# A decoder block on one core: VectorE issues in the order of the program text from step 40 to step 172

## The chip, the cores and the metric

The kernel runs on one core of one Trainium2 chip. Time is the device time of one execution in microseconds (us), taken over several executions; for the kernel before there are three, and one more that was profiled. The engines are named as the profile names them: PE is TensorE (PEld its weight loads), DVE is VectorE, ACT is ScalarE, POOL is GpSimd, SP is SyncE, whose queue issues most DMAs.

## The reference

One decoder layer on 256 tokens of width 2048, all in float32. The input is normalised and projected once; the projected columns feed two mixers that run side by side.

```python
h = rms_norm(x, g_mix); proj = h @ w_in                       # 2048 -> 8272 columns
u, z_ssm, c_q, k, v, z_attn, k_idx, w_idx, gate_ssm, gate_attn = split(proj)
y_ssm = s5_branch(u, ...) * silu(z_ssm)                        # diagonal complex state, a scan over 256 positions,
o_ssm = y_ssm @ w_ssm_out                                      #   then GELU and a gated projection (w_glu)
cq = rms_norm(c_q); q = cq @ w_uq; q_idx = cq @ w_uq_idx
y_attn = dsa_branch(q, k, v, q_idx, k_idx, w_idx) * silu(z_attn)   # 64 keys of 256 per query by an indexer's score
o_attn = y_attn @ w_attn_out
x = x + (sigmoid(gate_ssm) * o_ssm + sigmoid(gate_attn) * o_attn) @ w_o
x = x + sigmoid(rms_norm(x) @ w_ple_gate) * rms_norm(p @ w_ple)
return rms_norm(x, g_final)
```

## The kernel before, in words

**Units.** All weights stream through the core once. The stream is cut into 255 units of 128 partitions x 1024 columns (672 for eight of them), numbered in the order in which the products need them: 0 to 15 for `u`, 16 to 31 for `z_ssm`, 32 to 63 for `gate_ssm`, 64 to 79 for `z_attn`, 80 to 103 for three quarters of `gate_attn`, 104 to 115 for `c_q` and `k`, 116 to 123 for `v` and the indexer's key, 124 to 131 for `w_uq` and `w_uq_idx`, 132 to 147 for `w_glu`, 148 to 155 for the rest of `gate_attn`, 156 to 171 for `w_ssm_out`, from 172 for `w_attn_out`, and so on to `w_ple_gate`.

**Three products per weight.** A float32 product is made from three faster ones. A unit is loaded as `raw` by the SP queue (L99, five buffers). ACT rounds it to `hi` (`unit_hi`, L261, four buffers). DVE makes the remainder `lo` = `raw` - `hi` (`unit_lo`, L273, four buffers). PE then multiplies hi by hi, hi by lo and lo by hi into one accumulator (`mm3`, or `block_tm` with 512 columns per matmul: 12 matmuls per unit).

**One step per unit.** The main loop at L1225 writes step s in this order: the matmuls of unit s, `unit_hi(s + 3)`, the deferred evacuations of PSUM of earlier units (`run_deferred`), `unit_lo(s + 2)`, the load of the next unit, and then some work of the side threads (`pump(BUDGET)`, L33: about 1.3 us of DVE work per step by the threads' own estimates).

**The side threads** do what is no stream of weights. `s5_gen` (L939) is the scan: two halves of 16 state tiles each, `E[0]` in slot S7 and `E[1]` in slot S1. A half has 19 complex multiply-adds of four DVE instructions each (`cmadd`: L951, L953, L955, L957), so the scan has 152 DVE instructions. After a half, `s5_out` lets PE form the outputs (tile `aux`), DVE add the skip term (L998), ACT take the GELU (L1006) and round it (L1008), and DVE form the remainder (L1011). `attn_gen` scores keys (ACT L1034, DVE L1040 and L1042), picks 64 of them (L1049, L1050), forms logits (L1067) and their maximum (L1070), lets ACT take exponentials (L1073), divides on DVE (L1075, L1077), and at the end of it, head by head, multiplies with `za_d` loaded into `zld` (two buffers, L1104, L1086) and splits the product into hi and lo (ACT L1089, DVE L1092).

**Evacuations on DVE.** L438 scales a finished `z` block by the row of 1/rms; ACT then takes its SiLU (L442). L461, L470 and L472 do the same for `c_q`, L544 for the queries, L564, L566 and L568 for `w_glu`.

**What sets the order.** The program text only says what depends on what. A scheduler replays it with its own estimates of duration and writes one queue for each engine; each queue is then issued strictly in its order, with a semaphore wait where an operand comes from another engine. So an instruction that waits holds everything behind it on its engine. The scheduler may put a thread's DVE work far ahead of the step in which the text has it, and it did so with the scan.

Of the kernel before, what the change touches and what calls it, by code (L numbers as in the profile page):

```python
# [29 lines left out]
NC = 4  # L30
CW = 512
OFF = 16
NWARM = 30  # L33
BUDGET = 1.3
TRLAG = 2
# [9 lines left out]
def block_kernel(ctx: ExitStack, tc: tile.TileContext, A: dict, out: bass.AP):  # L45
# [18 lines left out]
    def slot(tag, shape, dt=F32):  # L64
        return cp.tile(shape, dt, tag=tag, name=nm(tag))

    def const(s, shape, dt=F32):
        return cp.tile(shape, dt, tag=s, name=s)
# [19 lines left out]
    def issue_unit(between=None):  # L88
        n = dma_next[0]
        if n >= len(units):  # L90
            return
        c, h, cols = units[n][:3]
        kind, idx = chunks[c]
        r = wp.tile([P, 1024], F32, tag="raw", name=nm("raw"), bufs=5)
        src = (A["wts"][idx] if kind == "w" else A["wvk"][idx])[:, h * cols:(h + 1) * cols]
        q = 2 if between else 1
        for i in range(q):
            s = slice(i * cols // q, (i + 1) * cols // q)
            nc.sync.dma_start(r[:, s], src[:, s])  # L99
            if between and i == 0:  # L100
                between()
        raws[n] = r
        dma_next[0] += 1
# [36 lines left out]
    def mm(o, l, r, start=True, stop=True, **kw):  # L140
        PE.matmul(o, l, r, start=start, stop=stop, **kw)  # L141
# [51 lines left out]
    def run_deferred(flush=False):  # L193
        while True:
            due = [d for d in deferred if flush or d[0] <= step[0]]
            if not due:
                return
            for d in due:
                deferred.remove(d)
            for d in due:  # L200
                d[1]()
# [26 lines left out]
    def pump(budget):  # L228
        credit[0] = min(credit[0] + budget, 3.0)
        while credit[0] > 0:  # L230
            ready = [t for t in threads if t[1] <= step[0]]
            if not ready:
                return
            credit[0] -= advance(ready[0])

    def drain(t):
        while not t[2]:
            advance(t)
# [13 lines left out]
    def unit_hi(u):  # L252
        if u >= len(units):
            return
        cols = units[u][2]
        hi = unit_tile("hi", u)
        src = raws[u][:, :cols]
        q = 2 if u < 3 else 1
        for i in range(q):
            o = slice(i * cols // q, (i + 1) * cols // q)  # L260
            S.copy(hi[:, o], src[:, o])  # L261
        his[u] = hi

    def unit_lo(u):
        if u >= len(units):
            return
        cols = units[u][2]
        lo = unit_tile("lo", u)
        src = raws.pop(u)
        q = 2 if u < 3 else 1  # L270
        for i in range(q):
            o = slice(i * cols // q, (i + 1) * cols // q)
            TT(lo[:, o], src[:, o], his[u][:, o].bitcast(F32), ALU.subtract)  # L273
        los[u] = lo
# [94 lines left out]
    def big_slot(tag, off=0):  # L369
        t = slot(tag, [P, KT * T + OFF], F32R)  # L370
        return t[:, off:off + KT * T].rearrange("p (k t) -> p k t", t=T)
# [254 lines left out]
    def ev_o(nb):  # L626
# [9 lines left out]
        def f(h, ps):  # L636
            if nb == 0 and h == 0:
                R["x2"] = slot("S1", [P, 2, D])
                R["x2h"] = big_slot("XH", OFF)
                R["x2l"] = big_slot("XL", OFF)  # L640
                R["sq2"] = const("sq2", [P, 2, NC])
# [373 lines left out]
    def attn_gen():  # L1015
# [63 lines left out]
        yield ("lag", 1)  # L1079
        ya = big_slot("S7", OFF).rearrange("p (c h) t -> p c h t", c=2)  # L1080
        R["ya"] = ya
# [128 lines left out]
    S.activation(first, mhalf, AF.Copy)  # L1210
    for i in range(NWARM):
        mm(wps[:, :T], warm[:, :P], warm)
# [9 lines left out]
    for i in range(2):  # L1222
        issue_unit()
    NU = len(units)
    for s in range(NU):  # L1225
        step[0] = s
        fn, need = units[s][3:]
        for n in need or ():
            if callable(n):
                n()  # L1230
            else:
                run_deferred()
                drain(R[n])
        fn(his.pop(s), los.pop(s))
        unit_hi(s + 3)
        run_deferred()
        unit_lo(s + 2)
        issue_unit()
        pump(BUDGET)
# [120 lines left out]
```

## Time and profile before

| what | value |
|---|---|
| three executions | 788.07, 788.10, 790.91 us (median 788.10) |
| the profiled execution | 790.16 us, of which the span from the first to the last instruction is 788.3 us |
| granted PE clock, mean over the span | 0.997 |
| PE busy | 766.6 us, 97% of the span |
| DVE busy | 576.5 us, 73% |
| ACT busy | 392.1 us, 50% |
| DMA, mean over the span | 201 GB/s |

A busy time is the union of the instructions of an engine. A matmul's record overlaps the next one's, so PE's busy time hides short losses; the distance from one matmul's start to the next tells more. "[2.27 <-DVE lo L273]" behind an instruction says that its engine was idle for 2.27 us before it, and that what ended the wait was an instruction of DVE at line 273 that writes `lo`.

### The profile page before, as it was taken

Reading aid. Unit: us, or ns where it says so; the run is one execution under the profiler, and the core shown is the slowest. Engines: PE = TensorE matmul, PEld = TensorE weight load, DVE = VectorE, ACT = ScalarE, POOL = GpSimd, SP = SyncE. Lnnn points to the kernel's source line nnn. Section 1 sums busy time; section 2 is a strip of 40 time slices with the busy share of each in tenths; the row PEclk is TensorE's granted clock in tenths of the full one; section 3 lists DMA queues with packets and bytes.
Section 4 is the critical chain, followed back from the end, with each engine's and each line's share of the span. In section 5 each row is a group of like instructions: output and inputs, shape, how many; then the busy total and the mean of one; then the engine's idle time right before and its main releaser. Section 6 shows DMA issues by size and latency. Waiting matters only on the chain.

```text
span 788.3 us, 12920 instructions
## 1 busy us (share of the span) xinstructions
PE 766.6 (97%) x5080; PEld 668.2 (85%) x5080; DVE 576.5 (73%) x902; ACT 392.1 (50%) x539; POOL 8.5 (1%) x18
## 2 busy tenths in 40 slices
PE   8999999999999899999999999999999999999995
PEld 6999987786998778899998987887888888888885
DVE  5999953999999964463768988665777855556753
ACT  7544456443433564453645474544446454455642
POOL 0000000000000000000000000000000000000000
PEclk9999999999999999999999999999999999999998
DMA  8768765355665376653664646775875765555622
GB/s 317 274 216 233 239 210 186 111 184 190 220 199 178 125 256 219 216 170 110 226 199 156 207 147 223 248 244 174 287 221 191 261 228 191 184 180 197 213 88 107
DMA packets 52637, 158.08 MB, mean 201 GB/s; under 512 B 5984, under 2 KB 12128, under 8 KB 52192
## 3 DMA queue, kind: packets, MB, share of 16 engines
q1 hardware_dynamic: 47392, 150.15, 57.9%
q10 hardware_dynamic: 5184, 7.10, 2.5%
q8 instruction: 40, 0.66, 0.4%
q14 instruction: 21, 0.17, 0.1%
HBM read 147.79 MB, written 8.39 MB: 198 GB/s over the span
## 4 chain that ended last, share of the span: by engine, by line
PE 47%; issue 1%; DMA 1%; DVE 1%; ACT 0%; POOLq 0%; POOL 0%; DVEq 0%
PE main L141 43%; PE aux L141 3%; PE aux L149 1%; DMA zld<-za_d 1%; DVE t L1086 0%; ACT S L669 0%; DVE S L667 0%; DVE S L668 0%; ACT S L664 0%; DVE S L671 0%; POOLq L1355 0%; POOL r3v L719 0%; DVE S L728 0%; DVEq L1355 0%; DVE S L726 0%
## 5 line engine op out<-in xcount | busy, mean ns | idle before, releaser
L273 DVE TENSOR_TENSOR lo<-raw,hi 128x1024 fp32r<-128x1024 f32 (+2 forms) x255 | 305.2, 1199 | 150.9 <-ACT hi L261 150.8
L261 ACT CAST hi<-raw 128x1024 fp32r<-128x1024 f32 (+2 forms) x255 | 261.6, 1033 | 285.4 <-PE main L141 240.0
L141 PE MATMUL main<-hi,S 128*128 128x512 f32 x512 | 162.6, 393 | 0.0
L141 PE MATMUL main<-lo,XH 128*128 128x512 f32 (+2 forms) x408 | 155.9, 382 | 5.5 <-DVE lo L273 5.5
L141 PE MATMUL main<-hi,XH 128*128 128x512 f32 (+2 forms) x408 | 157.0, 385 | 0.0
L141 PE MATMUL main<-hi,XL 128*128 128x512 f32 (+2 forms) x408 | 155.8, 382 | 0.0
L141 PE MATMUL main<-XH,lo 128*128 128x256 f32 x448 | 124.5, 278 | 1.6 <-DVE lo L273 1.5
L141 PE MATMUL main<-XH,hi 128*128 128x256 f32 x448 | 124.6, 278 | 0.0
L141 PE MATMUL main<-XL,hi 128*128 128x256 f32 x448 | 123.9, 276 | 0.0
L141 PEld LDWEIGHTS main<-hi,S 128*128 128x128 f32 x512 | 96.1, 188 | 19.3
L141 PE MATMUL main<-lo,S 128*128 128x512 f32 x256 | 99.9, 390 | 0.0
L141 PEld LDWEIGHTS main<-lo,XH 128*128 128x128 f32 x408 | 76.8, 188 | 22.2 <-DVE lo L273 8.2
L141 PEld LDWEIGHTS main<-hi,XH 128*128 128x128 f32 x408 | 76.7, 188 | 15.7 <-ACT t L555 0.5
L141 PEld LDWEIGHTS main<-hi,XL 128*128 128x128 f32 x408 | 76.7, 188 | 14.2
L141 PEld LDWEIGHTS main<-XH,lo 128*128 128x128 f32 x448 | 84.1, 188 | 2.8 <-DVE lo L273 2.8
L141 PEld LDWEIGHTS main<-XH,hi 128*128 128x128 f32 x448 | 84.2, 188 | 0.2
L141 PEld LDWEIGHTS main<-XL,hi 128*128 128x128 f32 x448 | 84.2, 188 | 0.1
L141 PE MATMUL main<-S,hi 128*128 128x256 f32 x384 | 67.1, 279 | 0.1
L141 PEld LDWEIGHTS main<-S,hi 128*128 128x128 f32 x384 | 58.1, 188 | 1.7 <-issue 0.7
L141 PEld LDWEIGHTS main<-lo,S 128*128 128x128 f32 x256 | 48.1, 188 | 9.4
L141 PE MATMUL main<-S,lo 128*128 128x256 f32 x192 | 53.1, 277 | 0.0
L141 PEld LDWEIGHTS main<-S,lo 128*128 128x128 f32 x192 | 36.1, 188 | 0.0
(222 smaller groups left out, 677.5 us busy)
## 6 DMA issues: line engine op xcount, KB each, us to landing
raw<-in_wts_dram SPq DMA_DIRECT2D x247, 512.0 KB, 4.3
raw<-in_wvk_dram SPq DMA_DIRECT2D x8, 336.0 KB, 2.9
gs_d<-big ACTq DMA_DIRECT2D x8, 256.0 KB, 3.2
ga_d<-big ACTq DMA_DIRECT2D x8, 256.0 KB, 5.0
big<-gs_d SPq DMA_DIRECT2D x8, 256.0 KB, 4.6
big<-ga_d SPq DMA_DIRECT2D x8, 256.0 KB, 4.4
S<-in_grow_dram SPq DMA_DIRECT2D x2, 1024.0 KB, 7.3
big<-in_xtok_dram SPq DMA_DIRECT2D x8, 256.0 KB, 3.6
```

The lines of the kernel that those rows point to most:

```text
L141: PE.matmul(o, l, r, start=start, stop=stop, **kw)
L149: PE.matmul(o, i, idn, is_transpose=True)
L261: S.copy(hi[:, o], src[:, o])
L273: TT(lo[:, o], src[:, o], his[u][:, o].bitcast(F32), ALU.subtract)
```

## The change

Between step 40 and step 172 of the main loop DVE is taken out of the scheduler's hands: its instructions stand in its queue in the order in which the program text emits them. ACT, PE, POOL and SP are still ordered by the scheduler. No instruction is added or taken away.

```diff
@@ -30,6 +30,7 @@
 OFF = 16
+FIXED = (40, 172)
 NWARM = 30
@@ -1222,8 +1223,14 @@
     NU = len(units)
+    order = None
     for s in range(NU):
         step[0] = s
+        if s == FIXED[0]:
+            order = ExitStack()
+            order.enter_context(tc.manual_schedule(engines={mybir.EngineType.DVE}))
+        if s == FIXED[1]:
+            order.close()
         fn, need = units[s][3:]
```

In the queues below every line of the program after the first added one has a number higher by one (L274 for L273). A name such as `lo_209` is the tile, and the number after it is the instruction that wrote it.

The DVE queue of before where the scan begins; `lo_204` to `lo_217` are units 43 to 46:

```order
L273 TENSOR_TENSOR lo_209_1818<-raw_184_1662,hi_203_1783 128x1024
L951 TENSOR_TENSOR S4_181_1645<-S7_185_1664,pre_106 128x1024
L953 TENSOR_TENSOR S4_181_1645<-S7_185_1664,psi_107 128x1024
L955 TENSOR_TENSOR S7_185_1664<-S7_185_1664,S4_181_1645 128x32x32
L273 TENSOR_TENSOR lo_213_1848<-raw_189_1692,hi_208_1816 128x1024
L957 TENSOR_TENSOR S7_185_1664<-S7_185_1664,S4_181_1645 128x32x32
L951 TENSOR_TENSOR S4_181_1645<-S7_185_1664,pre_106 128x1024
L953 TENSOR_TENSOR S4_181_1645<-S7_185_1664,psi_107 128x1024
L273 TENSOR_TENSOR lo_217_1878<-raw_194_1724,hi_212_1846 128x1024
```

The same place in the DVE queue of after:

```order
L274 TENSOR_TENSOR lo_204_1787<-raw_179_1634,hi_198_1753 128x1024
L952 TENSOR_TENSOR S4_181_1645<-S7_185_1664,pre_106 128x1024
L954 TENSOR_TENSOR S4_181_1645<-S7_185_1664,psi_107 128x1024
L956 TENSOR_TENSOR S7_185_1664<-S7_185_1664,S4_181_1645 128x32x32
L274 TENSOR_TENSOR lo_209_1820<-raw_184_1662,hi_203_1785 128x1024
L958 TENSOR_TENSOR S7_185_1664<-S7_185_1664,S4_181_1645 128x32x32
L274 TENSOR_TENSOR lo_213_1850<-raw_189_1692,hi_208_1818 128x1024
L952 TENSOR_TENSOR S4_181_1645<-S7_185_1664,pre_106 128x1024
L274 TENSOR_TENSOR lo_217_1880<-raw_194_1724,hi_212_1848 128x1024
```

Before, three scan instructions stand between two remainders from here on, which is where the scan's first half runs off; in the queue of after it is one or two, and the last scan instruction stands ahead of the remainder of unit 116, where before it stood ahead of that of unit 85.

The DVE queue of before around the skip terms of the first half (L998); `lo_353`, `lo_360`, `lo_367` and `lo_372` are units 80, 81, 82 and 83:

```order
L273 TENSOR_TENSOR lo_360_2958<-raw_334_2683,hi_351_2915 128x1024
L955 TENSOR_TENSOR S1_206_1789<-S1_206_1789,S4_181_1645 128x32x31
L957 TENSOR_TENSOR S1_206_1789<-S1_206_1789,S4_181_1645 128x32x31
L951 TENSOR_TENSOR S4_181_1645<-S1_206_1789,pre_106 128x32x31
L998 SCALAR_TENSOR_TENSOR t_355_2923<-S5_6_103,gains_78,aux_348_2787 128x256
L998 SCALAR_TENSOR_TENSOR t_356_2925<-S5_6_103,gains_78,aux_348_2787 128x256
L998 SCALAR_TENSOR_TENSOR t_357_2927<-S5_6_103,gains_78,aux_348_2787 128x256
L998 SCALAR_TENSOR_TENSOR t_362_2962<-S5_6_103,gains_78,aux_348_2787 128x256
L953 TENSOR_TENSOR S4_181_1645<-S1_206_1789,psi_107 128x32x31
L955 TENSOR_TENSOR S1_206_1789<-S1_206_1789,S4_181_1645 128x32x31
L273 TENSOR_TENSOR lo_367_2983<-raw_338_2717,hi_358_2953 128x1024
```

The same place in the DVE queue of after:

```order
L274 TENSOR_TENSOR lo_353_2921<-raw_329_2651,hi_344_2780 128x1024
L999 SCALAR_TENSOR_TENSOR t_355_2925<-S5_6_103,gains_78,aux_348_2789 128x256
L999 SCALAR_TENSOR_TENSOR t_356_2927<-S5_6_103,gains_78,aux_348_2789 128x256
L999 SCALAR_TENSOR_TENSOR t_357_2929<-S5_6_103,gains_78,aux_348_2789 128x256
L274 TENSOR_TENSOR lo_360_2960<-raw_334_2685,hi_351_2917 128x1024
L999 SCALAR_TENSOR_TENSOR t_362_2964<-S5_6_103,gains_78,aux_348_2789 128x256
L958 TENSOR_TENSOR S1_206_1791<-S1_206_1791,S4_181_1645 128x32x32
L439 TENSOR_TENSOR t_366_2983<-main_350_2892,row1_468 128x256
L274 TENSOR_TENSOR lo_367_2985<-raw_338_2719,hi_358_2955 128x1024
L952 TENSOR_TENSOR S4_181_1645<-S1_206_1791,pre_106 128x1024
L274 TENSOR_TENSOR lo_372_3010<-raw_343_2753,hi_365_2981 128x1024
```

Between the remainders of units 81 and 82 stood nine instructions (five of the scan, four skip terms), and the evacuation L438 came after the second; now it is one skip term, one scan instruction and the evacuation.

The DVE queue of before where the first query tile's exponentials come back from ACT; `lo_702`, `lo_709` and `lo_713` are units 149, 150 and 151:

```order
L273 TENSOR_TENSOR lo_702_5155<-raw_668_4945,hi_693_5104 128x1024
L566 TENSOR_TENSOR t_695_5109<-t_694_5107,zld_689_5069 128x256
L1075 RECIPROCAL sums1_677_4991<-sums1_677_4991 128x8
L1077 TENSOR_SCALAR S5_599_4555<-S5_599_4555,sums1_677_4991 128x256 x3
L273 TENSOR_TENSOR lo_709_5180<-raw_675_4987,hi_699_5148 128x1024
L1077 TENSOR_SCALAR S5_599_4555<-S5_599_4555,sums1_677_4991 128x256 x2
L564 TENSOR_TENSOR t_707_5176<-main_698_5123,t_700_5150 128x256
L568 TENSOR_TENSOR S3_606_4592<-t_695_5109,S3_606_4592 128x256
L566 TENSOR_TENSOR t_708_5178<-t_707_5176,zld_701_5152 128x256
L1077 TENSOR_SCALAR S5_599_4555<-S5_599_4555,sums1_677_4991 128x256 x3
L273 TENSOR_TENSOR lo_713_5214<-raw_684_5031,hi_706_5173 128x1024
```

The same place in the DVE queue of after:

```order
L274 TENSOR_TENSOR lo_702_5157<-raw_668_4947,hi_693_5106 128x1024
L569 TENSOR_TENSOR S3_606_4594<-t_695_5111,S3_606_4594 128x256
L565 TENSOR_TENSOR t_707_5178<-main_698_5125,t_700_5152 128x256
L567 TENSOR_TENSOR t_708_5180<-t_707_5178,zld_701_5154 128x256
L274 TENSOR_TENSOR lo_709_5182<-raw_675_4989,hi_699_5150 128x1024
L1076 RECIPROCAL sums1_677_4993<-sums1_677_4993 128x8
L1078 TENSOR_SCALAR S5_599_4557<-S5_599_4557,sums1_677_4993 128x256 x8
L274 TENSOR_TENSOR lo_713_5216<-raw_684_5033,hi_706_5175 128x1024
```

The `w_glu` remainder L568 (now L569), which needs ACT's rounding L567 of the same tile, moved from behind the remainder of unit 150 to ahead of it, and all eight divisions now stand between the remainders of units 150 and 151.

## Rows read from the trace of the kernel before

**Rows 1.** The page: span, and busy time of each engine (share, instructions).

```profile
span 788.3 us, 12920 instructions
PE 766.6 (97%) x5080; PEld 668.2 (85%) x5080; DVE 576.5 (73%) x902; ACT 392.1 (50%) x539; POOL 8.5 (1%) x18
```

**Rows 2.** Who waited for whom: us in total, times, longest us.

```profile
ACT big L442 <- DVE t L438: 48.2, 14, 4.6
...
PE main L141 <- DVE lo L273: 6.9, 8, 2.3
...
PE aux L149 <- DVE t L1086: 1.3, 1, 1.3
```

**Rows 3.** Busy us (instructions) by stretch: PE, PEld, DVE, ACT, POOL, clock, DMA.

```profile
137.00:180.00 43.00, 42.34 (x226) 33.45 (x225) 42.28 (x74) 19.74 (x25) 0.00 (x0) 1.00 0.43 146
180.00:220.00 40.00, 39.03 (x225) 33.46 (x224) 39.90 (x39) 17.21 (x19) 0.00 (x0) 1.00 0.63 210
220.00:260.00 40.00, 38.33 (x467) 35.79 (x466) 39.49 (x77) 14.49 (x19) 0.00 (x0) 1.00 0.56 178
260.00:284.00 24.00, 20.16 (x92) 16.09 (x91) 23.90 (x28) 15.59 (x20) 0.00 (x0) 1.00 0.49 158
284.00:360.00 76.00, 76.00 (x460) 67.44 (x459) 37.95 (x40) 36.71 (x43) 0.00 (x0) 1.00 0.66 214
300.00:320.00 20.00, 20.00 (x89) 16.39 (x88) 9.35 (x8) 8.64 (x9) 0.00 (x0) 1.00 0.66 220
```

**Rows 4.** DVE by line and shape, 284 to 360 us.

```profile
L273 DVE TENSOR_TENSOR lo<-raw,hi 128x1024 fp32r<-128x1024 f32 x27 | 33.1, 1225 | 33.8 <-ACT hi L261 33.7
```

**Rows 5.** PE in order of time, 266 to 275 us: start, us, instruction [idle before].

```profile
266.79 0.39 PE L141 MATMUL main<-hi,XH 128*128 128x512 f32 x1
269.45 0.49 PE L141 MATMUL main<-lo,XH 128*128 128x512 f32 x1 [2.27 <-DVE lo L273]
...
274.60 0.39 PE L141 MATMUL main<-hi,XL 128*128 128x512 f32 x1
274.83 0.39 PE L141 MATMUL main<-hi,XH 128*128 128x512 f32 x1
```

**Rows 6.** DVE in order of time, 259 to 268 us.

```profile
259.83 1.22 DVE L273 TENSOR_TENSOR lo<-raw,hi 128x1024 fp32r<-128x1024 f32 x1
260.97 1.19 DVE L955 TENSOR_TENSOR S<-S,S 128x992 f32<-128x992 f32 x1
...
264.40 1.65 DVE L998 SCALAR_TENSOR_TENSOR t<-S,gains,aux 128x256 f32<-128x256 f32 x4
...
268.17 1.22 DVE L273 TENSOR_TENSOR lo<-raw,hi 128x1024 fp32r<-128x1024 f32 x1
```

**Rows 7.** DVE by line and shape, 137 to 284 us: busy, mean ns | idle before.

```profile
L273 DVE TENSOR_TENSOR lo<-raw,hi 128x1024 fp32r<-128x1024 f32 x46 | 56.1, 1219 | 2.3 <-ACT hi L261 2.3
```

**Rows 8.** ACT in order of time, 456 to 465 us.

```profile
456.83 1.28 ACT L1073 ACT_TABLE_LOAD   x1
...
462.08 1.03 ACT L261 CAST hi<-raw 128x1024 fp32r<-128x1024 f32 x1
...
464.71 0.40 ACT L567 CAST S<-t 128x256 fp32r<-128x256 f32 x1
```

**Rows 9.** The chain that ended last, where units 150 and 151 run.

```profile
468.54 5.71 PE main L141 x24
```

**Rows 10.** DVE in order of time, at 462 us: three of the divisions.

```profile
462.45 0.88 DVE L1077 TENSOR_SCALAR S<-S,sums 128x256 f32<-128x256 f32 x3
```

**Rows 11.** All engines in order of time, 537 to 544 us: the heads' `zld`.

```profile
537.42 6.53 SPq L1104 DMA_DIRECT2D zld<-za_d  x4
...
542.70 0.76 DVE L1086 TENSOR_TENSOR t<-aux,zld 128x256 f32<-128x256 f32 x2 [3.37 <-DMA zld<-za_d]
...
543.18 0.55 PE L149 MATMUL aux<-ident,S 128*128 128x128 f32 x3 [1.29 <-DVE t L1086]
```

**Rows 12.** ACT in order of time, at 271 us.

```profile
270.86 0.42 ACT L442 ACTIVATE big<-t 128x256 f32<-128x256 f32 x1 [3.93 <-DVE t L438]
```

## The prediction

> **What bounds the kernel now.** I read the page's first part, then who waited for whom, then the busy times by stretch, then PE and DVE in order of time where PE stands still. PE is busy for 97% of the span and DVE for 73% [rows 1], so over the whole span only PE seems to count. The waits show what PE still loses: it waited for a remainder `lo` of DVE eight times, 6.9 us in all, and once for 1.3 us on the attention heads' L1086 [rows 2]. By stretch, the eight waits have one place. From 137 to 284 us DVE is busy for 42.28 + 39.90 + 39.49 + 23.90 = 145.6 of 147 us, and there PE is short by 0.66 + 0.97 + 1.67 + 3.84 = 7.1 us; from 284 to 360 us DVE is busy for 38 of 76 us and PE loses nothing [rows 3]. So one stretch is bound by DVE, the one in which the scheduler let the scan run off, and after it DVE has nothing to do but wait for ACT: 33.8 us before 27 remainders [rows 4]. The granted clock is 1.00 in every one of these stretches, the largest gap included [rows 3]: full clock, the higher of the two levels, so the gaps cost only their own length.
>
> Two readings of the same place: the longest gap ends at 269.45 [rows 5], and in DVE's order the remainder that PE wants starts at 268.17, 8.34 us after the one before it [rows 6]; between them stand the five scan instructions and four skip terms that the order of before shows between units 81 and 82.
>
> **The change part by part.** It adds and removes nothing. Its cost and its gain are in waits only.
>
> *The scan, units 44 to 116.* Work: 46 remainders [rows 7] at a distance of 1.14 us (259.83 to 260.97 [rows 6]) are 52.4 of the 145.6 us. Eight L438, four L998 and four L1011, each at the 0.41 us of an L998 (1.65 for four [rows 6]), are 6.6. The scan's 152 instructions thus cost about 86.6 us. Before, they ran beside the remainders of 42 units (44 to 85). After, by the order of the change, they end ahead of unit 116's remainder, so they are spread over 72 units: 86.6 / 72 = 1.20 us per unit, plus 1.14 for the remainder, plus 0.41 for an evacuation every second unit, 2.55 us. PE needs 12 x 0.23 = 2.76 us for a unit (274.60 to 274.83 [rows 5]). DVE is then the faster of the two all along, where before it needed 147 us for 46 remainders, 3.2 us each. The order has single units above PE's 2.76 (three scan instructions and a remainder in unit 44: 4 x 1.14 = 4.6 us), but in the text the remainder of unit s + 2 stands in step s, so it is two units early, 5.5 us, and the neighbours take 2.3. The cover is this lead; were it gone, each such unit would cost its excess, 1.8 us for unit 44 and under 1 us for the others.
>
> I therefore expect all eight waits to go. By idle time that is 6.9 us [rows 2]. By starts it is more: 266.79 to 269.45 is 2.66 us where 0.23 is due, a loss of 2.43 for an idle time of 2.27 [rows 5], because the modelled end of a matmul hides some of each gap. With 0.16 more for each of eight: 6.9 + 1.3 = 8.2 us. I take 8.2; the bounds are 6.9 and 8.4.
>
> The Trainium skill (Perfetto Trace Analysis, Identifying the Most-Contended Engine) holds matmul busy time for a poor measure, since matmuls overlap, and would have one use the share of weight loads. Against rows: at full rate with the same matmuls PEld is busy 16.39 of 20 us, a share of 0.82; in the last stretch it is 16.09 of 24 [rows 3]. By that measure this stretch lost 24 - 16.09 / 0.82 = 4.4 us, where idle time says 3.84. The sum by it would be about half a microsecond larger; it is not used further.
>
> *Waits that the new order adds.* An instruction at the head of DVE's queue that waits holds the remainders behind it. Three kinds stand ahead of a remainder now. First, evacuations (L438, L461, L564): they wait for a unit that PE has finished, and the remainder behind them is for two units later; 0.41 + 1.14 us against a lead of 5.5: nothing. Second, the skip terms and L1011, which wait for `s5_out` on PE and for ACT. PE does `s5_out` at one go after unit 77, when DVE has written the remainders up to unit 80; three skip terms and the next remainder take 1.2 + 1.1 us after it while PE has three units to do. L1011 waits for ACT, whose casts wait for PE to free a buffer; by ACT's durations (a table load 1.28 us, a cast 1.03, a rounding 0.40 [rows 8]) the remainders come 2 us or more before they are due. I take nothing; if it fails, a cast's 1.03 us per L1011, eight of them. Third, the exponentials: L568 now stands ahead of unit 150's remainder and waits for L567, which ended at 465.1 [rows 8], behind eight exponentials, a cast and a table load. Then L564, L566, L568 and the remainder take 3 x 0.41 + 1.14 = 2.4, and the remainder is there at 467.5; PE starts unit 150 at 468.54 [rows 9], a slack of 1.0. The eight divisions (0.88 for three [rows 10], so 2.3) and the next remainder end at 470.9; unit 151 starts 5.71 / 2 = 2.9 us after unit 150, at 471.4, a slack of 0.5. I take 0; the bounds are 0 and 1.5.
>
> *The heads' `zld`, units 172 to 174.* Here DVE waited 3.37 us for loads that SP issued at 537.42, and PE 1.29 us behind it [rows 11]. In the new order SP issues the loads in two lots, tied to the L1086 that frees each buffer, and the second head's L1086 now stands behind two more remainders or evacuations. It can take the 1.3 us away, or add one more DVE wait less the cover PE has for it, 3.37 - 1.3 = 2.1. I take + 0.4, the middle.
>
> *What becomes of it.* After 560 us nothing that PE waits for is moved, and PE has no idle time to soak up a gain, so it arrives at the end. ACT waited 48.2 us for L438 [rows 2], 3.93 in the worst region before a SiLU with the casts queued behind it [rows 12]; the evacuations come sooner now, which only helps. The loads of `raw` are issued when a remainder frees a buffer; DMA is busy for 0.43 to 0.66 of these stretches [rows 3], with five buffers, so they follow.
>
> Sum: the profiled execution took 790.16 us (span 788.3, and 1.9 around it). 790.16 - 8.2 + 0 + 0.4 = 782.4. The median of the three executions stands 2.06 under the profiled one, at 788.10; the forecast is 788.1 - 7.8 = 780.3 us, 1.0% faster.
>
> **The rivals.** *The gain is half eaten.* ACT stays in an order that was planned by estimates; where DVE's queue now waits for ACT (L1011, L568, L1075) and ACT's casts wait for PE, lateness goes round. With half of the eight casts' 1.03 us exposed and the two slacks of unit 150 and 151 missed by 1 us each, 4 + 2 = 6 us come back: about 786. For it: the slacks are 0.5 to 2 us, small. Against: only waits ahead of a remainder count, and PE lost nothing there before with similar ones.
>
> *Nothing happens.* The volume on DVE is unchanged. If PE's gaps are set by the chain hi, lo, matmul and not by the queue, they stay: 788.1. The Trainium skill (same page and section) has one improve the engine with the highest occupancy first; by that rule, read over the span, an order on DVE at 73% would be worth nothing. Against it, the stretches: DVE at 99% exactly where PE waits [rows 3].
>
> *Slower.* One mechanism: the queue loses its lead. The scheduler put remainders first whenever they could run; now every remainder waits for whatever the text has before it. If DVE arrives at its evacuations a unit late, the lead of two units is one, and each place at which it also waits for ACT (eight L1011, eight L568, eight score groups) exposes a cast of 1.03 us: 24 x 1.03 = 24.7, less the 8.2, is + 16.5, 805 us. It decides from 12 such places on. For it: DVE at 2.55 of 2.76 us has only 8% to catch up. Against: the lead of 5.5 us is longer than any one row in the new order but one.
>
> **How the numbers follow.** Forecast 0.70, half eaten 0.12, nothing 0.10, slower 0.08. What a measurement of this kernel can tell from no change is about 0.5%, 784.2 to 792.0. Of the forecast's own range, 778.5 to 784.5, nearly all lies below that; of the half-eaten case a fifth, so faster is 0.70 + 0.03 = 0.73 and, with some of the forecast lost to slacks, I say 0.75; the same 0.16, slower 0.09. The low end is 788.1 - 8.4 - 1.3 = 778.4; the high end takes in most of the half-eaten case, 786.8.
>
> **What would show it.** Right: DVE busy for 0.85 to 0.93 from 137 to 350 us instead of 0.99 and then 0.50; no PE wait on `lo` between 170 and 280 us; L438 waits of ACT down by more than half. Wrong: a PE gap before unit 81 to 88, 119 to 124 or 150 to 152 that ends on a `lo` (the second kind of wait, or the third), or a gap above 1.3 us at the heads. If the eight gaps go and the time doesn't, the gain was lost after 360 us.

## The result, and the profile after

| | before | changed | ratio |
|---|---|---|---|
| executions, us | 789.0 median (788.07 to 790.91, 4) | 779.69 median (779.49 to 780.15, 4) | 0.9885, 95% interval 0.9872 to 0.9899 |
| the profiled execution, us | 790.16 | 779.49 | |
| start of PE's 1201st matmul (ahead of unit 44), us | 145.89 | 144.30 | |
| from there to the start of the last matmul, us | 633.13 | 624.44 | 8.69 less |

The kernel is 1.15% faster; 780.3 us was forecast. The last two rows are worked out from the starts of the 5080 matmuls that both traces hold, matched by number (61 of them, in four places, stand in a slightly different order, since the scheduler ordered PE anew). They matter below: the time up to unit 44, which the change does not touch, differs by up to 1.9 us between profiled executions, and the second span does not have that in it.

(The text ahead counts 255 units. 255 is the number of pieces: the first three units come in two pieces each, so there are 252 units. The unit numbers used here and there are not touched by this.)

The changed kernel's page, to set beside [rows 1]:

```profile
span 777.7 us, 12910 instructions
PE 765.5 (98%) x5080; PEld 670.5 (86%) x5080; DVE 575.3 (74%) x902; ACT 392.2 (50%) x539; POOL 9.3 (1%) x18
```

Every engine has the same instructions to work on, and PE's idle time is 12.2 us where it was 21.7. Who waited for whom, in PE's answer (us in total, times, longest): no remainder `lo` is in it any more, against eight waits in [rows 2].

```profile
PE aux L150 <- DVE t L1087: 0.4, 1, 0.4
...
PE main L142 <- ACT t L556: 0.3, 1, 0.3
```

And of all engines, the waits that stand for the evacuations (ACT's were 48.2 us in [rows 2]) and for a place that the prediction did not have:

```profile
ACT big L443 <- DVE t L439: 17.0, 6, 3.5
...
DVE kb L487 <- PE aux L142: 10.7, 1, 10.7
```

Busy times by stretch, columns as in [rows 3]:

```profile
137.00:180.00 43.00, 43.00 (x231) 34.59 (x230) 36.86 (x43) 20.30 (x24) 0.00 (x0) 1.00 0.53 177
180.00:220.00 40.00, 40.00 (x251) 35.81 (x250) 34.34 (x59) 19.68 (x22) 0.00 (x0) 1.00 0.67 218
220.00:260.00 40.00, 40.00 (x468) 37.34 (x467) 31.30 (x36) 18.46 (x23) 0.00 (x0) 1.00 0.55 180
260.00:284.00 24.00, 24.00 (x107) 19.69 (x106) 22.45 (x26) 15.21 (x20) 0.00 (x0) 1.00 0.66 221
284.00:320.00 36.00, 36.00 (x163) 29.68 (x162) 31.96 (x62) 15.92 (x18) 0.00 (x0) 1.00 0.67 215
```

PE is busy throughout, DVE for 0.78 to 0.94 of every stretch where it was at 0.98 to 1.00 and then at 0.50. The matmul behind the longest gap of [rows 5], the same one by number, now starts 0.23 us after the one ahead of it:

```profile
258.74 0.39 PE L142 MATMUL main<-hi,XH 128*128 128x512 f32 x1
258.97 0.39 PE L142 MATMUL main<-lo,XH 128*128 128x512 f32 x1
```

**Where the 8.69 us are.** The difference of the two kernels' starts, matmul by matmul, moves in five places:

| stretch of the changed kernel | gain, us |
|---|---|
| units 44 to 85: the eight waits, what hangs on them, and 0.5 at a stop of PE near the end of the scan's outputs | +10.85 |
| units 104 to 115: 256-column matmuls 0.118 us apart, before 0.113 | -1.30 |
| units 124 to 147: the same, -1.63; a wait for ACT's L533 gone, +0.37 | -1.26 |
| around unit 148: a wait for ACT's L556 | -0.22 |
| units 172 to 174, the heads | +0.63 |

So the scan was worth more than the whole, and 2.9 us of it were given back by PE itself, later on and without a wait. In 25 us that hold such matmuls alone, the kernel before (335 to 360 us: instructions | busy us, mean ns of one) had 223 of them:

```profile
L141 PE MATMUL main<-XL,hi 128*128 128x256 f32 x75 | 20.7, 276 | 0.0
L141 PE MATMUL main<-XH,lo 128*128 128x256 f32 x74 | 20.4, 276 | 0.0
L141 PE MATMUL main<-XH,hi 128*128 128x256 f32 x74 | 20.4, 276 | 0.0
```

The changed kernel (325 to 350 us) has 214, at a granted clock of 1.00 and without idle time in either:

```profile
L142 PE MATMUL main<-XH,hi 128*128 128x256 f32 x72 | 20.2, 281 | 0.0
L142 PE MATMUL main<-XL,hi 128*128 128x256 f32 x71 | 20.0, 281 | 0.0
L142 PE MATMUL main<-XH,lo 128*128 128x256 f32 x71 | 20.0, 281 | 0.0
```

### The profile page after: what moved, and what is told of

Read it like the earlier page. It is cut to its first block, busy times and chain, and to the rows that moved or that the text cites. A ratio compares the mean times of both kernels' runs of the same rounds, so it can differ in the third digit from the quotient of the medians.

```text
span 777.7 us, 12910 instructions
## 1 busy us (share of the span) xinstructions
PE 765.5 (98%) x5080; PEld 670.5 (86%) x5080; DVE 575.3 (74%) x902; ACT 392.2 (50%) x539; POOL 9.3 (1%) x18
## 4 chain that ended last, share of the span: by engine, by line
PE 87%; DVE 6%; issue 3%; DMA 2%; ACT 2%; SPq 0%; POOLq 0%; POOL 0%; DVEq 0%
PE main L142 79%; PE aux L142 7%; DVE lo L274 2%; DMA raw<-in_wts_dram 1%; PE aux L150 1%; DVE S L859 1%; DVE S L857 1%; DMA zld<-za_d 1%; ACT XH L385 1%; DVE S L855 0%; ACT hi L262 0%; ACT S L393 0%; PE small L142 0%; ACT S L1074 0%; DVE S L413 0%
## 5 line engine op out<-in xcount | busy, mean ns | idle before, releaser
L274 DVE TENSOR_TENSOR lo<-raw,hi 128x1024 fp32r<-128x1024 f32 (+2 forms) x255 | 304.1, 1196 | 99.5 <-ACT hi L262 99.0
```

## The experiments

Two numbers are used throughout. The first is the span from PE's 1201st matmul to its last, as above (before 633.13, changed 624.44). The second is the lead of a remainder: from the end of its record on DVE to the start of the first matmul that reads it. Where it is 0.05 to 0.1 us PE was waiting. Both are worked out from the traces. Leads in us:

```
unit                     53    60    70    77    85    116   140   150   151
before                  0.05  1.19  0.06  0.06  0.68 13.24  7.28  4.35  3.65
changed                 5.96  5.96  3.91  3.93  1.92  0.19  3.28  1.55  0.83
one unit less (lead1)   5.96  5.95  1.67  1.19  1.21  1.91  0.06  0.19  0.23
dense scan              0.06  0.06  0.05  0.06  5.95  4.65  2.95  1.55  0.83
range to 148            5.96  5.96  3.91  3.93  1.92  0.19  3.28  4.57  3.88
```

**Which part of the range brings it.**

```diff
-FIXED = (40, 172)
+FIXED = (40, 120)
```

> The range ends at step 120 instead of 172, so only the scan and the evacuations beside it are in the order of the text. My theory, that the gain comes from the scan being spread over units 44 to 116: the eight PE waits on a remainder between 137 and 284 us are gone, the attention heads' wait of 1.3 us is back (1.47 us between starts in the kernel before against 0.67 in the changed one), and the time is 780 to 781.5 us, 0.9884 to 0.991 of the kernel before. Rival, that the range from 120 on brings most of it (evacuations, exponentials, heads): 786 to 788 us. Beside it, the 256-column matmuls, which in the profile of the changed kernel stood 0.118 us apart from 319 to 445 us and 0.113 us before and in the kernel before: if that belongs to the order of DVE, it is here too, since the queues are alike up to unit 119; if it is a state of an execution, it may be absent, and the time is then up to 2.8 us less.

780.12 us median (779.34 to 781.43), ratio 0.989 (0.9875 to 0.9906), span 624.42: as the changed kernel. PE's waits on a remainder are gone, and it waits 0.9 us at the heads. The scan's part of the range is the gain.

```diff
-FIXED = (40, 172)
+FIXED = (120, 172)
```

> The range begins at step 120, so the scan is left to the scheduler and only what comes after it is in the order of the text. My theory: the eight PE waits on a remainder stay, 6.9 us of idle time, the heads gain 0.8 us, the small wait before unit 148 costs 0.4: 787.5 to 789 us, no difference from the kernel before that can be measured. Rival, that the later range brings most of the gain: 780 to 782 us.

788.75 us median (788.52 to 789.94), ratio 0.9999 (0.999 to 1.0009), span 633.77. PE's answer of the waits has the old ones back:

```profile
PE main L142 <- DVE lo L274: 7.0, 7, 2.9
PE aux L150 <- DVE t L1087: 1.3, 1, 1.3
```

The range from 120 on is worth nothing. It did not gain the 0.8 us at the heads that I had given it either.

**Order or load.** Is it the order of the text that helps, or that it thins out the scan?

```diff
-        pump(BUDGET)
+        pump(2 * BUDGET if 40 <= s < 120 else BUDGET)
```

> As the changed kernel, but from step 40 to 119 each step takes twice the side work (2.6 in place of 1.3 us by the threads' estimates), still in the order of the text. In the queue of DVE the scan then ends ahead of unit 81's remainder, where it ends ahead of unit 116's in the changed kernel. My theory, that DVE's work per unit against PE's 2.75 us decides: 86.6 us of scan, 37 remainders at 1.14 and some 7 of evacuations and skip terms are 136 us for 37 units that take PE about 110 us with the outputs of the scan; less two units of lead (5.5) PE waits for remainders for about 20 us between 135 and 260 us, and the time is 795 to 803 us, slower than the kernel before by 1 to 2%. Rival, that the order of the text as such brings the gain (a remainder in every row, evacuations early): 779 to 782 us. Second rival, that PE's gaps are set by the chain hi, lo, matmul: 779 to 782 us too.

799.43 us median (799.17 to 799.9), ratio 1.0134 (1.0119 to 1.0149), span 644.52, 20.1 us over the changed kernel where about 20 were worked out. PE waits 20 times, and DVE is full again (PE, PEld, DVE busy by stretch):

```profile
PE main L142 <- DVE lo L274: 13.9, 20, 1.5
```

```profile
137.00:180.00 43.00, 41.81 (x223) 32.95 (x222) 42.25 (x74) 19.24 (x23) 0.00 (x0) 1.00 0.43 143
180.00:220.00 40.00, 35.71 (x333) 27.34 (x332) 39.79 (x39) 16.21 (x18) 0.00 (x0) 1.00 0.46 154
220.00:260.00 40.00, 34.19 (x274) 32.12 (x272) 39.11 (x78) 19.23 (x26) 0.00 (x0) 1.00 0.49 167
```

An order of the text at twice the side work is slower than the scheduler's. Both rivals (order as such; a chain of hi, lo and matmul that no queue changes) fall: what counts is DVE's work per unit against PE's 2.75 us.

**The lead.**

```diff
-        unit_lo(s + 2)
+        for d in () if s == 40 else (1,) if 40 < s < 172 else (1, 2) if s == 172 else (2,):
+            unit_lo(s + d)
```

> As the changed kernel, but in the range step s writes the remainder of unit s + 1 and not s + 2, so a remainder has one unit of lead (2.75 us) instead of two (5.5 us); the rate of side work is the same. My theory, that the lead covers single rows above PE's 2.75 us: the row with three scan instructions (4.6 us) now costs about 1.8 us, the rows with an evacuation that waits for the end of the unit before, 0.41 + 1.2 + 1.14 = 2.75 and no slack, cost some tenths each, and each of the eight places where DVE waits for ACT up to 1 us: 784 to 792 us. Rival, that only the mean rate counts (2.55 against 2.75 us per unit) and the lead hides nothing: 779.5 to 780.5 us.

784.31 us median (783.47 to 785.41), ratio 0.9943 (0.9927 to 0.9959), span 628.85: 4.4 us lost, inside the forecast, but not where I had put it. The row with three scan instructions left unit 43 a lead of 2.6 us and cost nothing, and from unit 49 to 65 the leads are those of the changed kernel (table). The distance in the text sets the lead only from unit 67 on, where evacuations in DVE's queue wait for a unit that PE has finished: 1.2 to 1.7 us at units 67 to 73, where the changed kernel has 3.9 to 4.4 from unit 68 on. Ahead of that nothing in DVE's queue waits for PE but buffers, so that DVE works ahead in either (this reason is read from the queue, no run tried it). The losses, matched by starts with the changed kernel, are of several kinds. Some 1.7 us came where DVE waits for ACT on top, as the "slower" rival has it. First 0.8 us at unit 84, DVE at 260 us,

```profile
260.64 0.42 DVE L1012 TENSOR_TENSOR S<-t,S 128x256 fp32r<-128x256 f32 x1 [1.20 <-ACT S L1009]
...
264.78 0.43 DVE L1012 TENSOR_TENSOR S<-t,S 128x256 fp32r<-128x256 f32 x1 [1.44 <-ACT S L1009]
...
266.25 1.22 DVE L274 TENSOR_TENSOR lo<-raw,hi 128x1024 fp32r<-128x1024 f32 x1
```

and PE right behind that remainder:

```profile
267.53 0.50 PE L142 MATMUL main<-lo,XH 128*128 128x512 f32 x1 [0.50 <-DVE lo L274]
```

Then 0.9 in units 148 to 151, where the first query tile's exponentials keep ACT busy and the `w_glu` remainder waits for it (the changed kernel has the same wait of 5.04 us, and there the lead covers it):

```profile
459.07 0.42 DVE L569 TENSOR_TENSOR S<-t,S 128x256 fp32r<-128x256 f32 x1 [5.04 <-ACT S L568]
```

Another 1.1 us was lost at unit 140. DVE waits for nothing there, but has 2.8 us of key picking (L1050, L1051) between two remainders, so this is a single row above PE's 2.75 us, as my theory had it, only not the row that I had named:

```profile
429.14 0.39 PE L142 MATMUL main<-S,lo 128*128 128x256 f32 x1 [0.79 <-DVE lo L274]
```

And 1.1 us is not shown to have to do with the lead. PE stopped near the end of the scan's outputs, at a matmul at which the kernel before also stops (0.16 us), and the profile has no wait for it; the rest of the 4.4 us is in small pieces:

```profile
249.50 0.42 PE L142 MATMUL aux<-S,S 128*32 128x31 f32 x6 [0.84 <-issue]
```

Nine of the remainders of units 44 to 171 have a lead under 0.1 us here, none in the changed kernel, twelve in the kernel before.

**The given-back 2.9 us.** First the changed kernel again, as it is.

> The changed kernel itself once more, with a second profile, beside the three variants of it that follow. Its 256-column matmuls stood 0.118 us apart from 319 to 445 us, where the kernel before has 0.113: 26 units of 24 matmuls, 0.11 us each, 2.8 us. Theory A, that the rate belongs to the program: PE never pauses between 150 and 450 us, so it enters each row of 256-column matmuls in the same phase in every execution: again 0.118 from 319 to 445 us. Theory B, that it is chance: other stretches this time. The time is 779.5 to 780.2 us either way.

780.51 us median (780.2 to 781.47), 0.3 us over the forecast; span 624.49. From unit 104 on the rate is the same at the same matmuls: 0.118 us from entering unit 104 to 404 us, and in pieces to 444, as theory A has it. But the program alone does not set the rate. Units 64 to 73 of the kernel before ran at 0.113, and in the profile of the kernel before with the cut alone (a run further down, whose cut stands behind these units) the same instructions in the same order ran at 0.118. From 209 to 223 us, the kernel before:

```profile
L141 PE MATMUL main<-XH,lo 128*128 128x256 f32 x42 | 11.6, 276 | 0.0
```

and that run:

```profile
L142 PE MATMUL main<-XH,lo 128*128 128x256 f32 x41 | 11.5, 281 | 0.0
```

```diff
         mm(o, wh, ah, start=start, stop=False)
-        mm(o, wh, al, start=False, stop=False)
+        if step[0] in CUT and start:          # CUT = (104, 124)
+            for c in range(2):
+                mm(o[:, c * P:(c + 1) * P], wh, al[:, c * P:(c + 1) * P], start=False, stop=False)
+        else:
+            mm(o, wh, al, start=False, stop=False)
```

> As the changed kernel, but in the first group of products of unit 104 and in the first of each of the two blocks of unit 124 the second matmul is cut in two of 128 columns; nothing else is moved. It costs three short matmuls, some 0.1 us each. Theory A, that the phase in which PE enters a row of 256-column matmuls without a pause decides between 0.113 and 0.118 us a matmul until the next pause: the cut breaks the phase, and the rate is 0.113 behind unit 104 or behind unit 124 or both, 1.3 us (12 units) and up to 1.5 us less, less 0.3 for the cut: 777.3 to 779.3 us. Rival, that something beside PE sets the rate there (DMA, what DVE writes): 0.118 as before, 779.8 to 780.4 us.

(Below this run is called f1_cut.) 777.09 us median (776.94 to 777.27), ratio to the kernel before 0.9848 (0.9833 to 0.9863), and below every execution of the changed kernel on the same chip. Span 621.29, 3.15 less; 2.5 of it lie between unit 104 and 148, 0.6 at the heads. PE's matmuls, 325 to 350 us, are 223 again:

```profile
L143 PE MATMUL main<-XH,hi 128*128 128x256 f32 x75 | 20.7, 276 | 0.0
L143 PE MATMUL main<-XL,hi 128*128 128x256 f32 x74 | 20.4, 276 | 0.0
L143 PE MATMUL main<-XH,lo 128*128 128x256 f32 x74 | 20.4, 276 | 0.0
```

With the cut, unit 104 was entered at 0.113 here and in the next run; without it, at 0.118 in all five profiles in which PE did not pause ahead of it. So a change in PE's own matmuls is enough to bring the faster rate, while DMA and DVE are given the same work as before. This is the version that beats both kernels.

> The changed kernel with the cut at unit 104 alone. Theory A (the phase at entry holds until PE pauses or the kind of matmul changes): 0.113 from 320 us to the end of the 256-column matmuls of units 104 to 115, 1.3 us less the 0.1 of the cut, and 0.118 again in the row that begins with unit 124: 778.3 to 779.5 us, about 1 us under the changed kernel and over f1_cut. Rival, that one cut sets the rate for all that follows: 777 us as with both.

(The diff is that of f1_cut with `CUT = (104,)`.) 779.49 us median (777.93 to 781.34), ratio 0.9868 (0.9846 to 0.9891), span 622.36: 2.1 us under the changed kernel, where 1.2 were expected. The executions lie far apart, and by their interval this run can't be told from the changed kernel (0.9872 to 0.9899); what follows is from the profiled one, 777.93 us. Between unit 104 and 148 it gains 2.3 against 2.5 with both cuts; the rest of the difference is the heads. Behind unit 104 the rate is 0.113; in the row that begins with unit 124 it is 0.118 again, as expected, but only up to two transposes in the midst of it, and 0.113 behind them (PE, starts 0.35 us apart for three matmuls ahead of them and 0.34 behind):

```profile
388.07 0.28 PE L143 MATMUL main<-S,lo 128*128 128x256 f32 x1
388.19 0.40 PE L143 MATMUL main<-S,hi 128*128 128x256 f32 x2
388.42 0.28 PE L143 MATMUL main<-S,lo 128*128 128x256 f32 x1
388.55 0.38 PE L155 MATMUL small<-ident,kin 128*128 128x128 f32 x2
...
389.70 0.28 PE L143 MATMUL main<-S,lo 128*128 128x256 f32 x1
389.81 0.39 PE L143 MATMUL main<-S,hi 128*128 128x256 f32 x2
390.04 0.28 PE L143 MATMUL main<-S,lo 128*128 128x256 f32 x1
```

So a break can change the rate, and not always for the better: in the scan-only run (range to 120) PE paused at 377 us and ran at 0.113 from there, and the same two transposes took it back to 0.118; so it did in the run with ACT in the order of the text, below. At unit 104 the kernel before, the run with the range from 120 on and the dense run, all with pauses up to 270 us or later, come out at 0.113; the five without pauses at 0.118; the run with one unit less, which paused for 0.50 us at 267 us, at 0.118 too. That pauses put PE on the faster rate is thus a guess that fits most of these profiles, and not shown.

The cut alone, in the kernel before:

> The kernel before with the cut alone (units 104 and 124, as in f1_cut), without the order of the text. In its profile the 256-column matmuls run at 0.113 us from 332 to 364 us and from 388 us on already; PE paused for 1.6 us at 277 us. Theory A, that the eight pauses of the kernel before put PE back to the faster rate and that the changed kernel, which takes them away, gives back 2.8 us so: the cut has nothing to win here beyond the 0.9 us that is at 0.118 in the profile, and costs 0.3: 787.5 to 789.5 us, the same as the kernel before. Rival, that the cut is worth 3 us in any order: 785 to 786.3 us.

788.75 us median (788.01 to 790.53), ratio 0.9982 (0.997 to 0.9995), span 632.97 against 633.13. By the interval it may be 0.05 to 0.3% better; the spans say 0.2 us, and between unit 104 and 148, where the cuts are, it lost 0.3. Not the 3 us that it is worth in the changed kernel: PE is on the faster rate there already. The rival (a cut helps in any order) falls. Nor do pauses always bring the faster rate: behind the first three of them, at 177 to 185 us, this run and the one with the range from 120 on entered unit 64 at 0.118, and the kernel before at 0.113.

**The end of the range, and ACT.**

```diff
-FIXED = (40, 172)
+FIXED = (40, 148)
```

> The range ends at step 148: the exponentials, the divisions and the heads go back to the scheduler's order. My theory, that this part is worth nothing: the remainders of units 150 and 151, which in the changed kernel were written 1.55 and 0.83 us before PE needed them, have 3 us or more again, the PE wait of 0.26 us on L556 goes, and the heads' PE wait is back (1.47 us between starts against 0.67): 779.7 to 780.7 us. Rival, that the range to step 172 is worth something by itself (divisions in one lot, loads in time): 781 to 783 us.

781.02 us median (779.96 to 781.63), ratio 0.9896 (0.9881 to 0.9912), span 624.08. The median is 0.3 us over my forecast and on the edge of the rival's, but 0.5 over the repeated changed kernel, whose executions (780.2 to 781.47) it overlaps; by the span it is 0.4 us shorter. So no difference is shown. Units 150 and 151 have their lead back (table), and PE had not waited for them anyway. The wait on L556 stayed (0.27 us), against what I expected; the heads cost 0.4 us less, not more.

```diff
-                order.enter_context(tc.manual_schedule(engines={mybir.EngineType.DVE}))
+                order.enter_context(tc.manual_schedule(engines={mybir.EngineType.DVE, mybir.EngineType.Activation}))
```

> As the changed kernel, but ACT too is in the order of the text from step 40 to 172; the queues of PE, DVE and SP stay as they are. In ACT's queue a cast hi now mostly stands ahead of the SiLU or evacuation beside it. My theory, that PE is bound by its own work there (it waits for nothing but 0.9 us in all): the same, 779.3 to 780.3 us, and the remainders come no later. Rival, that an order on ACT planned for another order on DVE costs: the casts come sooner, the smallest lead (0.19 us at unit 116, 0.83 at unit 151) grows, and 1 to 2 us come back: 777.5 to 778.7 us. Second rival, the text's order makes ACT wait in front of casts: 781 us or more.

780.0 us median (779.86 to 781.57), ratio 0.9889 (0.9873 to 0.9905), span 624.62: the same. The smallest leads did not grow (0.18 at unit 116, 0.84 at 151). That ACT stayed in the scheduler's order neither cost nor brought anything.

## Why the prediction was right, point by point

- **DVE bounds one stretch, PE the rest: right.** The dense run shows it from the other side, and the two halves of the range show the place.
- **The eight waits, 8.2 us by starts: right to the digit, and not the whole.** Matched matmul by matmul they are 0.83 + 0.82 + 0.47 + 0.33 + 0.86 + 0.76 + 2.43 + 1.73 = 8.23. The stretch gave 10.85. Not priced were the matmul behind each wait, which also starts 0.11 us late (0.9), two more remainders that came just too late without being among the eight waits and one matmul ahead of them (0.8), 0.5 near the end of the scan's outputs, where PE stopped for 0.16 us without a wait that the profile shows, and steps under 0.1. The Trainium skill's share of weight loads (Perfetto Trace Analysis, Identifying the Most-Contended Engine) made the last stretch 4.4 us where idle time made it 3.84; by starts it was 4.39. The trace agrees with the page there. It does so only against a share of like matmuls: from 180 to 220 us, where 256-column matmuls come in as well, the same sum gives 40 - 33.46 / 0.82 = -0.8, and the starts 1.6.
- **Nothing after it that costs PE: wrong, by 2.9 us.** "PE has no idle time to soak up a gain, so it arrives at the end" is the step that failed. A PE without idle time still has two rates for the same matmul, and in the changed kernel it took the slower one from unit 104 on; that the missing pauses are the reason is not shown. Of the 8.69 us by starts the forecast had 7.8. Not in it were + 2.65 (above), - 2.93 (the rate), + 1.03 (the heads), + 0.37 (L533) and - 0.22 (L556). That the two large ones cancel is luck. (The medians moved by 9.3 us; the fourth execution of the kernel before put its median from the 788.10 of the forecast to 789.0.)
- **2.55 us of DVE work per unit against 2.76: right** (DVE busy for 182.37 of 213 us from 137 to 350, 0.86; 0.85 to 0.93 was said).
- **The lead of 5.5 us: right in size, wrong in kind.** It was 5.96 at units 53 and 60, and there the text's order does not set it; where it does, it was 3.9 at units 70 and 77.
- **Waits that the new order adds: nothing, right, with one place missed.** Units 150 and 151 were given slacks of 1.0 and 0.5 us and had 1.55 and 0.83. The tightest place is one that I did not name: L486 (now L487) waits at the head of DVE's queue while PE does the outputs of the second half, and the remainder of unit 116 behind it was there 0.19 us before PE wanted it.

```profile
347.62 0.41 DVE L473 TENSOR_TENSOR acc<-acc,t 128x256 f32<-128x256 f32 x1
358.73 0.42 DVE L487 TENSOR_TENSOR kb<-main,row 128x256 f32<-128x256 f32 x1 [10.70 <-PE aux L142]
359.07 1.61 DVE L274 TENSOR_TENSOR lo<-raw,hi 128x672 fp32r<-128x672 f32 x2
```

- **The heads: + 0.4 forecast, - 0.6 measured.** The wait is shorter, to answer [rows 11]:

```profile
530.65 0.42 DVE L1087 TENSOR_TENSOR t<-aux,zld 128x256 f32<-128x256 f32 x1 [1.12 <-DMA zld<-za_d]
...
531.13 0.55 PE L150 MATMUL aux<-ident,S 128*128 128x128 f32 x3 [0.42 <-DVE t L1087]
```

  It is no property of the range: with the range from 120 on it was 1.3 us, with the range to 120 0.9, and in f1_cut PE does not wait there at all. What sets it was not settled.
- **The profiled execution against the median: right to be set apart.** 1.59 us of the 10.67 between the two profiled executions lie ahead of unit 44.
- **The rivals.** Nothing happens: excluded by the two halves of the range. Half eaten: the loss was of half that size, but on PE and not between DVE and ACT. Slower: its mechanism exists, with one unit of lead in place of two, and then costs some 1.7 of the 4.4 us, not 25.

## What to carry to other kernels

Read idle time by stretch before asking which engine bounds: side work that a scheduler runs off at once can bind for a fifth of the time an engine that is idle half of the next fifth, and spreading it at a rate below the bound is what an order by hand gives, as a denser order by hand shows. Price a wait by the distance of the starts around it, the next matmul included. And when the last waits of PE go, compare the distance of like matmuls in both traces: a full PE can still run at two rates, and not always at the same one when the same instructions run again.

## What the runs showed of the hardware that was not expected

- A row of 128x256 matmuls, each with its own weight load, ran 0.1133 or 0.1178 us apart (24 in 2.72 or 2.83 us), without idle time and at a granted clock of 1.00 in both, and kept its rate, but for the first few matmuls, until PE paused, met matmuls of another kind, or had one cut in two. From unit 104 on the two profiles of the changed kernel agree in the rate of every such row. Elsewhere the same row of the same program took either: the row that begins at 22 to 24 us, far ahead of the change, ran at 0.113 in nine of the twelve profiles and at 0.118 in three. Which rate it takes was settled by nothing here beyond that. 128x512 matmuls showed one rate: 24 of them in 5.49 us in both kernels.
- Up to unit 44 profiled executions of the same instructions took from 144.22 to 146.12 us.
